# A two-layer streaming trunk on one core: output weight's sums tied to score steps one by one, and the final norm of a row block in two pieces

## The chip, the cores and the metric

The kernel runs on one core of a Trainium2 chip. The metric is the device time of one execution in microseconds, as a median over runs. Before the change it is 2714.26 us (three runs, 2712.99 to 2715.75). Matrix products run on TensorE (PE; its weight loads, PEld, are listed apart), elementwise work on VectorE (DVE), ScalarE (ACT) and GpSimd (POOL). Every DMA is issued by SyncE (SP), in the order of its queue.

## The reference

`x` has 2048 rows of 1024 numbers, all in float32. Layer A is a gated MLP with spatial mixing. Layer B, where the change lies, is attention of each 64-row chunk over its own and the eight chunks before it, with a bias by relative position, a SiLU gate and an output projection. A last RMS norm gives the result:

```
q, z = split(rms_norm(x, b_g) @ w_qz);   k, v = split(rms_norm(x, kv_g) @ w_kv)
p    = softmax(q k^T / 8 + bias[rel])    # per chunk of 64 rows, band of 576
o    = (p v) * silu(z)
x2   = x + o @ w_b_out
out  = x2 * rsqrt(mean(x2^2) + 1e-6) * final_norm_g
```

## The kernel before

**Tiling.** Layer B walks over four tiles t of 512 rows and, in each, over eight head pairs p (two heads of 64). One (t, p) has eight **steps** u = 0 to 7: two heads times four blocks of 128 query rows. Every product in float32 accuracy is made of three passes over a high and a low part (`mm3`, L112 to L116), so operands have to be split: ACT copies the high part, DVE subtracts it to get the low part.

**One step.** `score` (L1299) of a step two further on: PE multiplies queries with keys (L1314), DVE adds the bias and takes the row maximum (L1322), ACT takes the exponential (L1329), DVE the reciprocal of the sum (L1332), POOL scales the row (L1333). `flip` (L1338) of this step: PE transposes the five 128-column blocks of the row into the one PSUM buffer `tp` (L1349; its pool `ptr` has one buffer), ACT casts them into the high part of `pt` (L1352), DVE subtracts to the low part (L1353). Only then can PE transpose the next row. At two places of a pair `value` (L1358) multiplies the probabilities with the values. In tile 0 a row has 128 to 512 columns, from tile 1 on 640, so that the first 640-wide cast of L1352 is step 0 of tile 1, pair 0.

**What fills PE between the steps.** A generator (`ahead`, L1577) gives projections of the next pair and parts of the output projection of the tile before (`o_all`, L1552), in shares per pair (`SHARE`, L1558). The output projection is a Strassen-like product: seven phases, each with a weight matrix that is a sum or difference of quarters of the output weight.

**The sums of the output weight.** `o_sums` (L289) makes these seven matrices once, during tile 1, pairs 0 to 3 (a quarter of the columns in each pair). It loads four pieces `wo` (L296) and returns seven functions; the main loop calls one per step, at u = 0 to 6, just behind `flip` (L1637). Each calls `keep` (L299): ACT copies the high part (L303), DVE subtracts the low part (L304), SP stores both to DRAM (`ows`, L306; one phase also stores `owf`, L301). The first three also run sums on POOL: two (L310, L311), one (L315), one (L319). The high and low parts lie in a pool of four buffers (tag "S"), so two phases fit at once. The output projection of tile 0, from pair 4 on, reads `ows` (L231).

**The final norm.** When a 128-row block of x2 is complete, `done` (L1488) leaves a `finish` (L1504) in the list `finals`; the main loop calls the first one in each step with u > 0 (L1635), behind `flip`. `finish` adds two partial sums of squares (L1507), takes the inverse root (L126 to L128, on DVE and POOL), loads the block `y` from DRAM (L1513; the tag "bx" has one buffer), scales its two halves on DVE (L1516) and stores them (L1520). There are four such blocks for each of tiles 0, 1 and 2, finished in tiles 1, 2 and 3. For the last tile the rows stay on the chip and `finish` runs at once.

**What sets the order.** The lines above only say in which order instructions are written. When the program is built, the framework plans each engine's queue: with its own estimates of durations it puts an instruction into the queue as soon as its inputs and buffers are free by the plan, the earliest written one first. An instruction can so stand far ahead of where it was written. On the chip each queue runs strictly in the planned order and waits on semaphores for what it needs. A manual dependency without a semaphore (`NoSync`; `paced_by_pj`, L173, is one already) binds the plan alone: the instruction isn't placed before the named one is done by the plan.

Of the kernel before, what the change touches and what calls it, by code (L numbers as in the profile page):

```python
# [13 lines left out]
ALU = mybir.AluOpType  # L14
# [3 lines left out]
P = 128  # L18
# [3 lines left out]
T = 512  # L22
# [11 lines left out]
def trunk_kernel(  # L34
# [19 lines left out]
    nc = tc.nc  # L54
# [27 lines left out]
    ident = cst.tile([P, P], F32, name="ident")  # L82
# [27 lines left out]
    mm, tpose = nc.tensor.matmul, nc.tensor.transpose  # L110
# [12 lines left out]
    sub, add = ALU.subtract, ALU.add  # L123
    tv, tg = nc.vector.tensor_tensor, nc.gpsimd.tensor_tensor

    def root(r):  # L126
        nc.vector.tensor_scalar(r, r, EPS, None, op0=ALU.add)
        nc.gpsimd.tensor_tensor(r, r, mhalf[:], op=ALU.pow)  # L128
# [40 lines left out]
            tv(tl[:, :, b * P : (b + 1) * P], x3, oh.bitcast(F32), op=sub)  # L169

    pace = []

    def paced_by_pj(ins):  # L173
        if pace:
            tc.add_manual_dep(
                ins.ins, pace[-1],
                mybir.DependencyInfo(mybir.DependencyClass.NoSync, mybir.DependencyReason.DATA),
                reason="order",
            )
# [109 lines left out]
    def o_sums(u, place, s_place):  # L289

        q, i = divmod(u, 2)
        cs = slice(i * 512, i * 512 + 512)
        w = {}
        for rc in ((0, 0), (0, 1), (1, 1), (1, 0)):
            w[rc] = place(f"wo{u}_{rc[0]}{rc[1]}")
            paced_by_pj(nc.sync.dma_start(w[rc][:], wb_out[rc[0], rc[1], q][:, cs]))  # L296
        b11, b12, b21, b22 = (w[k][:] for k in ((0, 0), (0, 1), (1, 0), (1, 1)))

        def keep(ph, src):  # L299
            if ph == 5:  # L300
                nc.sync.dma_start(owf[q][:, cs], src)  # L301
            hi, lo = (s_place(f"so{u}_{ph}{x_}") for x_ in "hl")
            nc.scalar.copy(hi[:], src)  # L303
            tv(lo[:], src, hi[:].bitcast(F32), op=sub)  # L304
            for n, y_ in enumerate((hi, lo)):
                nc.sync.dma_start(ows[ph, q][:, n, cs], y_[:].bitcast(F32))  # L306

        def first():
            keep(1, b11)
            tg(b11, b12, b11, op=sub)  # L310
            tg(b12, b22, b12, op=sub)  # L311

        def second():
            keep(3, b22)
            tg(b22, b22, b11, op=sub)  # L315

        def third():
            keep(2, b21)
            tg(b21, b21, b22, op=sub)  # L319

        return [first, second, third] + [
            lambda ph=ph, o=o: keep(ph, o)
            for ph, o in ((5, b11), (7, b12), (6, b22), (4, b21))
        ]

    with ExitStack() as actx:
# [21 lines left out]
        sub, add, mul = ALU.subtract, ALU.add, ALU.mult  # L348
# [7 lines left out]
        last = {}  # L356
# [536 lines left out]
        for n in range(2, 6):  # L893
            b = start[n, 1]
# [46 lines left out]
        tv, tg = nc.vector.tensor_tensor, nc.gpsimd.tensor_tensor  # L941
# [259 lines left out]
    with ExitStack() as bctx:  # L1201
# [5 lines left out]
        gf = cb.tile([P, D], F32, name="gf")  # L1207
# [10 lines left out]
        def half_tile(tag, name, bufs, dtype=F32):  # L1218
            return sb.tile([P, 512], dtype, tag=tag, name=name, bufs=bufs)

        def c_tile(name):
            return half_tile("C", name, 4)
# [115 lines left out]
        def flip(t, p, u):  # L1338

            hd, qb = divmod(u, 4)  # L1340
            h = 2 * p + hd
            if qb == 0:
                pts[t, h] = sb.tile([P, 5376], F32R, tag="PT", name=f"pt{t}_{h}", bufs=1)
            pt = pts[t, h]
            pr = prs[t, h, qb]
            b0 = 0 if t > 0 else 4 - qb
            tp = ptr.tile([P, KD, P], F32, tag="tr", name=f"tp{t}_{h}_{qb}")
            for b in range(b0, 5):
                tpose(tp[:, b, :], pr[:, b * P : (b + 1) * P], ident[:])  # L1349
            o = qb * 640  # L1350
            oh = pt[:, o + b0 * P : o + 640]
            nc.scalar.copy(oh, tp[:, b0:5, :].rearrange("p a b -> p (a b)"))  # L1352
            nc.vector.tensor_tensor(  # L1353
                pt[:, 2560 + o + b0 * P : 2560 + o + 640],
                tp[:, b0:5, :].rearrange("p a b -> p (a b)"), oh.bitcast(F32), op=ALU.subtract,
            )
# [40 lines left out]
        finals = []  # L1397
# [74 lines left out]
        def o_evict(t):  # L1472
            xa, ya = {}, {}
            last = t + 1 == NT

            def resid(r, c, jp, x_):
                b = 2 * jp + r
                nc.sync.dma_start(x_, x1d[t][b * P : (b + 1) * P, c * 512 : c * 512 + 512])

            def place(r, c, jp):  # L1480
                if not last:
                    return c_tile(f"oc{t}_{r}{c}{jp}")[:]
                b = 2 * jp + r
                if b not in row:
                    row[b] = sb.tile([P, 2, 512], F32, tag="K", name=f"row{b}", bufs=4)
                return row[b][:, c, :]

            def done(r, c, jp, y):  # L1488
                b = 2 * jp + r
                if (t, b) not in ssq:  # L1490
                    ssq[t, b] = sm.tile([P, 2], F32, tag="ssq", name=f"ssq{t}_{b}", bufs=4)
                jk = c_tile(f"jk{t}_{r}{c}{jp}")
                nc.scalar.activation(
                    jk[:], y, AF.Square, scale=1.0 / 32, accum_out=ssq[t, b][:, c : c + 1]
                )
                if not last:
                    nc.sync.dma_start(x2d[t][b][:, c * 512 : c * 512 + 512], y)
                if (r, c) in ((1, 0), (0, 1)):
                    if last:
                        finish(b)  # L1500
                    else:
                        finals.append(lambda: finish(b))

            def finish(b):  # L1504
                r = sm.tile([P, 1], F32, tag="rr", name=f"rr_f{t}_{b}", bufs=4)
                s_ = ssq[t, b]
                tv(r[:], s_[:, 0:1], s_[:, 1:2], op=add)  # L1507
                root(r[:])
                if last:
                    y = row[b]  # L1510
                else:
                    y = sb.tile([P, 2, 512], F32, tag="bx", name=f"y{t}_{b}", bufs=1)
                    nc.sync.dma_start(y[:].rearrange("p a b -> p (a b)"), x2d[t][b][:])  # L1513
                for c in range(2):
                    cs = slice(c * 512, c * 512 + 512)
                    nc.vector.scalar_tensor_tensor(  # L1516
                        y[:, c, :], y[:, c, :], r[:], gf[:, cs], op0=ALU.mult, op1=ALU.mult
                    )
                    r0 = t * T + b * P
                    nc.sync.dma_start(out[r0 : r0 + P, cs], y[:, c, :])  # L1520

            def evict(ph, jp, ps):
                if ph in (1, 7):
                    d = xa if ph == 1 else ya
                    d[jp] = half_tile("U", f"ou{t}_{ph}_{jp}", 4)[:]
                    nc.scalar.copy(d[jp], ps)
                    return
                x_, y_ = xa[jp], ya[jp]
                if ph in (2, 5):
                    r = 0 if ph == 2 else 1  # L1530
                    c = place(r, r, jp)
                    resid(r, r, jp, c)
                    tv(c, ps, c, op=add)
                    tg(c, c, x_ if ph == 2 else y_, op=add)
                    done(r, r, jp, c)
                    if ph == 5:
                        tv(x_, ps, x_, op=add)
                        for r, c, y in ((1, 0, y_), (0, 1, x_)):
                            o = c_tile(f"or{t}_{r}{c}{jp}")[:]
                            resid(r, c, jp, o)  # L1540
                            tg(y, y, o, op=add)
                elif ph == 6:
                    tv(x_, ps, x_, op=add)
                    tg(y_, y_, x_, op=add)
                else:
                    r, c, y = (1, 0, y_) if ph == 4 else (0, 1, x_)
                    o = place(r, c, jp) if last else y
                    tv(o, ps, y, op=add)  # L1548
                    done(r, c, jp, o)
            return evict  # L1550
# [53 lines left out]
        first = ahead(0, 0)  # L1604
# [102 lines left out]
```

## Time and profile before

| | before |
|---|---|
| median of three runs | 2714.26 us |
| the profiled execution | 2716.97 us |
| its span, first to last instruction | 2715.2 us |
| mean granted TensorE clock | 0.988 |
| instructions | 38098 |

Times in the profile count from the start of the span. A row of the timeline gives the start, the duration, engine, line, operation, output and inputs, shapes, and in brackets the idle time of the engine just before, with what ended it. Attention takes the span from about 1540 us on; tile 1 begins near 1764 us, tile 2 near 2082 us, tile 3 near 2378 us.

### The profile page before, as it was taken

The page shows a single profiled execution, that of the slowest core. Times are in us where ns is not written, and L with a number is a line of the kernel's source. Part 1 is how long each engine was busy: PE and PEld are TensorE (multiplying, and loading weights), DVE is VectorE, ACT ScalarE, POOL GpSimd, SP SyncE. Part 2 cuts the span into 40 slices and gives each one's busy share as a digit, 9 for nine tenths or more (in the row PEclk, how much of TensorE's full clock was granted, in tenths as well). Part 3 has the DMA queues.
Part 4 walks back from the last instruction along what each step waited for, and adds up shares of the span by engine and source line. Part 5 has one row for each costly group of instructions (what it writes and reads, how often), then busy time and mean ns, then how long its engine had stood idle before and what let it go on. Part 6 is the DMA issues. An engine that isn't in the chain of part 4 may idle for free. (4 is left out here: it accounts for less than half of the span.)

```text
span 2715.2 us, 38098 instructions
## 1 busy us (share of the span) xinstructions
PE 2630.3 (97%) x12960; PEld 2195.9 (81%) x12960; DVE 1891.3 (70%) x2937; ACT 1296.8 (48%) x2296; POOL 892.1 (33%) x874
## 2 busy tenths in 40 slices
PE   9999999999999999999989999999999999999997
PEld 7788888888888888888878777787887888888875
DVE  6655676676677768667687666778667667766676
ACT  5422242433524435332365465666555565665553
POOL 3512235142351414114134243333332223223243
PEclk9999999999999999999999999999999999999999
DMA  8898999989988879768666677788778667766577
GB/s 302 309 334 333 349 354 328 328 308 352 325 308 299 294 263 344 252 222 298 241 215 226 210 255 222 233 287 272 260 261 286 213 211 239 243 205 198 182 228 244
DMA packets 274770, 735.53 MB, mean 271 GB/s; under 512 B 29584, under 2 KB 61328, under 8 KB 274576
## 3 DMA queue, kind: packets, MB, share of 16 engines
q1 hardware_dynamic: 274576, 733.09, 77.9%
q8 instruction: 104, 1.70, 0.3%
q14 instruction: 90, 0.74, 0.1%
HBM read 540.56 MB, written 181.93 MB: 266 GB/s over the span
## 5 line engine op out<-in xcount | busy, mean ns | idle before, releaser
L113 PE MATMUL P<-T,S 128*128 128x512 f32 x1248 | 495.2, 397 | 2.1 <-ACT S L376 2.1
L115 PE MATMUL P<-T,S 128*128 128x512 f32 x1248 | 489.3, 392 | 0.0
L114 PE MATMUL P<-T,S 128*128 128x512 f32 x1248 | 488.1, 391 | 0.6 <-DVE T L379 0.6
L1333 POOL TENSOR_SCALAR pr<-pr,sl 128x640 f32<-128x640 f32 (+4 forms) x256 | 198.2, 775 | 564.7 <-DVE sl L1332 494.5
L113 PE MATMUL pj<-hh_b,wh_b 128*128 128x512 f32 x768 | 322.2, 419 | 1.8 <-ACT hh_b L168 1.0
L115 PE MATMUL pj<-hh_b,wl_b 128*128 128x512 f32 x768 | 305.6, 398 | 0.3 <-DVE wl_b L200 0.2
L114 PE MATMUL pj<-hl_b,wh_b 128*128 128x512 f32 x768 | 305.6, 398 | 0.0
L1329 ACT ACTIVATE pr<-pr,nm 128x640 f32<-128x640 f32 (+4 forms) x256 | 195.4, 763 | 176.5 <-DVE nm L1322 170.8
L115 PEld LDWEIGHTS P<-T,S 128*128 128x128 f32 x1248 | 234.7, 188 | 50.2
L113 PEld LDWEIGHTS P<-T,S 128*128 128x128 f32 x1248 | 235.3, 189 | 46.8 <-ACT S L376 2.3
L114 PEld LDWEIGHTS P<-T,S 128*128 128x128 f32 x1248 | 235.2, 188 | 46.3 <-DVE T L379 1.0
L1353 DVE TENSOR_TENSOR pt<-tp,pt 128x640 fp32r<-128x640 f32 (+4 forms) x256 | 188.9, 738 | 60.1 <-ACT pt L1352 56.7
L1322 DVE CUSTOM_DVE_ANT_0 pr<-s,bias 128x640 f32<-128x640 f32 (+4 forms) x256 | 188.3, 735 | 38.5 <-PE s L1314 33.0
L1349 PE MATMUL tp<-ident,pr 128*128 128x128 f32 x1120 | 169.2, 277 | 26.9 <-DVE pt L1353 23.2
L1352 ACT CAST pt<-tp 128x640 fp32r<-128x640 f32 (+4 forms) x256 | 159.2, 622 | 64.5 <-PE tp L1349 60.4
L1349 PEld LDWEIGHTS tp<-ident,pr 128*128 128x128 f32 x1120 | 131.7, 142 | 62.6 <-issue 30.4
L115 PEld LDWEIGHTS pj<-hh_b,wl_b 128*128 128x128 f32 x768 | 146.1, 190 | 33.6 <-DVE wl_b L200 1.2
L1373 PEld LDWEIGHTS pv<-pt,V 128*128 128x128 f32 x896 | 144.9, 191 | 29.0 <-DVE pt L1353 7.9
L1373 PE MATMUL pv<-pt,V 128*128 128x256 f32 (+3 forms) x896 | 157.7, 323 | 7.3 <-DVE pt L1353 4.3
L113 PEld LDWEIGHTS pj<-hh_b,wh_b 128*128 128x128 f32 x768 | 147.1, 191 | 20.3 <-ACT wh_b L199 1.6
L114 PEld LDWEIGHTS pj<-hl_b,wh_b 128*128 128x128 f32 x768 | 147.1, 192 | 16.9
L200 DVE TENSOR_TENSOR wl_b<-raw_b,wh_b 128x1024 fp32r<-128x1024 f32 x96 | 122.8, 1280 | 33.2 <-ACT wh_b L199 32.0
(284 smaller groups left out, 5734.5 us busy)
## 6 DMA issues: line engine op xcount, KB each, us to landing
S<-hsd SPq DMA_DIRECT2D x288, 512.0 KB, 5.3
rw<-in_w_a SPq DMA_DIRECT2D x108, 512.0 KB, 6.2
A<-ytd SPq DMA_DIRECT2D x72, 512.0 KB, 5.8
raw_b<-wk SPq DMA_DIRECT2D x72, 512.0 KB, 4.3
hsd<-S SPq DMA_DIRECT2D x56, 512.0 KB, 4.4
V<-vhd SPq DMA_DIRECT2D x56, 512.0 KB, 5.2
wh_bo<-ows SPq DMA_DIRECT2D x50, 512.0 KB, 4.5
wl_bo<-ows SPq DMA_DIRECT2D x50, 512.0 KB, 5.6
```

Source lines behind the costliest of these rows:

```text
L113: first = mm(ps, lh, rh, start=first, stop=False)
L114: mm(ps, lh, rl, start=False, stop=False)
L115: mm(ps, ll, rh, start=False, stop=last)
L200: tv(wl[:], raw[:], wh[:].bitcast(F32), op=sub)
L1322: nc.vector.tensor_tensor_reduce(out=pr[:, c0:].rearrange("p (a b) -> p a b", a=nseg), in0=ps[:, :nseg, :w], in1=bias[:, c0:].rearrange("p ...
L1329: nc.scalar.activation(pr[:, c0:], pr[:, c0:], AF.Exp, scale=-1.0, bias=nm[:], accum_out=sl[:])
L1333: nc.gpsimd.tensor_scalar(pr[:, c0:], pr[:, c0:], sl[:], 1.0, op0=ALU.mult, op1=ALU.mult)
L1349: tpose(tp[:, b, :], pr[:, b * P : (b + 1) * P], ident[:])
L1352: nc.scalar.copy(oh, tp[:, b0:5, :].rearrange("p a b -> p (a b)"))
L1353: nc.vector.tensor_tensor(pt[:, 2560 + o + b0 * P : 2560 + o + 640], tp[:, b0:5, :].rearrange("p a b -> p (a b)"), oh.bitcast(F32), op=ALU ...
L1373: mm(po[:, q0 * P : q1 * P], vtl[t, p][:, i, hs], rhs, start=(i == blocks[0] and j == 0), stop=(i == 7 and j == 1),)
```

## The change

A list `beat` gets the name of the last transposition of each `flip`. `on_beat` gives an instruction a dependency without a semaphore on the newest entry: it isn't placed in its queue before that transposition is done by the plan. So tied are, in the sums, the ACT copy of each `keep` and the four POOL sums; the DVE subtraction and the stores follow from their data. In the final norm, for tiles 0 to 2, `finish` is cut in two: the addition (tied), the root and the load of `y` in one step, and the two scalings (tied) with their stores as a function `scale` that is put at the head of `finals`, and so called in the next step with u > 0. The load of `y` is not tied. For the last tile nothing changes. No instruction is added or taken away.

```
+    beat = []
+    def on_beat(ins):
+        if beat:
+            tc.add_manual_dep(
+                ins.ins, beat[-1],
+                mybir.DependencyInfo(mybir.DependencyClass.NoSync, mybir.DependencyReason.DATA),
+                reason="order",
+            )
+        return ins
...
-            nc.scalar.copy(hi[:], src)
+            on_beat(nc.scalar.copy(hi[:], src))
...
-            tg(b11, b12, b11, op=sub)
-            tg(b12, b22, b12, op=sub)
+            on_beat(tg(b11, b12, b11, op=sub))
+            on_beat(tg(b12, b22, b12, op=sub))
...
-                tpose(tp[:, b, :], pr[:, b * P : (b + 1) * P], ident[:])
+                ins = tpose(tp[:, b, :], pr[:, b * P : (b + 1) * P], ident[:])
+            beat.append(ins.ins.name)
...
-                tv(r[:], s_[:, 0:1], s_[:, 1:2], op=add)
+                first = tv(r[:], s_[:, 0:1], s_[:, 1:2], op=add)
                 root(r[:])
                 if last:
                     y = row[b]
                 else:
+                    on_beat(first)
                     y = sb.tile([P, 2, 512], F32, tag="bx", name=f"y{t}_{b}", bufs=1)
                     nc.sync.dma_start(y[:].rearrange("p a b -> p (a b)"), x2d[t][b][:])
-                for c in range(2):
...
+                def scale():
+                    for c in range(2):
+                        cs = slice(c * 512, c * 512 + 512)
+                        ins = nc.vector.scalar_tensor_tensor(
+                            y[:, c, :], y[:, c, :], r[:], gf[:, cs], op0=ALU.mult, op1=ALU.mult
+                        )
+                        if not last:
+                            on_beat(ins)
+                        r0 = t * T + b * P
+                        nc.sync.dma_start(out[r0 : r0 + P, cs], y[:, c, :])
+
+                if last:
+                    scale()
+                else:
+                    finals.insert(0, scale)
```

The two POOL sums of the second and third function (L315, L319) are tied in the same way.

More of the change, by code (lines that the diff above doesn't have):

```diff
@@ L309, in first @@
             keep(1, b11)
-            tg(b11, b12, b11, op=sub)
-            tg(b12, b22, b12, op=sub)
+            on_beat(tg(b11, b12, b11, op=sub))
+            on_beat(tg(b12, b22, b12, op=sub))
         def second():
             keep(3, b22)
-            tg(b22, b22, b11, op=sub)
+            on_beat(tg(b22, b22, b11, op=sub))
         def third():
             keep(2, b21)
-            tg(b21, b21, b22, op=sub)
+            on_beat(tg(b21, b21, b22, op=sub))
         return [first, second, third] + [
@@ L1511, in finish @@
                 else:
+                    on_beat(first)
                     y = sb.tile([P, 2, 512], F32, tag="bx", name=f"y{t}_{b}", bufs=1)
                     nc.sync.dma_start(y[:].rearrange("p a b -> p (a b)"), x2d[t][b][:])
-                for c in range(2):
[L1515 to L1520, printed above, removed]
+                def scale():
[12 more added lines that the diff above has]
+                    finals.insert(0, scale)
             def evict(ph, jp, ps):
```

## The prediction

> **What bounds the kernel now.** I read the page first, for the engine that is the bound, then the waits of that engine, then the timeline of the engines that it waits for.
>
> ```profile
> span 2715.2 us, 38098 instructions
> PE 2630.3 (97%) x12960; PEld 2195.9 (81%) x12960; DVE 1891.3 (70%) x2937; ACT 1296.8 (48%) x2296; POOL 892.1 (33%) x874
> L1349 PE MATMUL tp<-ident,pr 128*128 128x128 f32 x1120 | 169.2, 277 | 26.9 <-DVE pt L1353 23.2
> ```
>
> PE is the bound, busy for 97%. What can be won is its idle time, and in attention most of that stands before transpositions: there is one buffer `tp`, so a transposition waits until DVE has taken the row before out of it (L1353). Two stretches matter here, PE's waits while the sums are made (1735 to 1900 us) and while tile 1's final blocks are written (2290 to 2400):
>
> ```profile
> PE tp L1349 <- DVE pt L1353: 9.1, 4, 3.2
> ```
>
> ```profile
> PE tp L1349 <- DVE pt L1353: 6.0, 2, 3.1
> PE s L1314 <- DVE nm L1322: 0.6, 1, 0.6
> ```
>
> The sums cost 9.1 us in four gaps, the final blocks 6.0 in two and a remainder. The timeline has the larger five, and the windows of 6 us around each have the clock in the column behind the engines:
>
> ```profile
> 1805.55 0.52 PE L1349 MATMUL tp<-ident,pr 128*128 128x128 f32 x3 [2.11 <-DVE pt L1353]
> 1840.66 0.66 PE L1349 MATMUL tp<-ident,pr 128*128 128x128 f32 x2 [2.54 <-DVE pt L1353]
> 1877.23 0.41 PE L1349 MATMUL tp<-ident,pr 128*128 128x128 f32 x2 [3.18 <-DVE pt L1353]
> 2308.51 0.87 PE L1349 MATMUL tp<-ident,pr 128*128 128x128 f32 x3 [2.93 <-DVE pt L1353]
> 2345.06 0.41 PE L1349 MATMUL tp<-ident,pr 128*128 128x128 f32 x2 [3.11 <-DVE pt L1353]
> ```
>
> ```profile
> 1805.00:1811.00 6.00, 5.45 (x23) 4.71 (x24) 4.17 (x9) 2.30 (x5) 1.09 (x3) 0.72 0.96 311
> 1839.00:1845.00 6.00, 4.34 (x17) 3.87 (x18) 4.50 (x9) 2.63 (x5) 0.91 (x2) 0.72 0.76 221
> 1876.00:1882.00 6.00, 4.77 (x18) 4.13 (x19) 4.36 (x9) 1.87 (x4) 0.80 (x1) 0.72 0.67 210
> 2307.00:2313.00 6.00, 4.49 (x18) 3.96 (x19) 5.91 (x11) 2.21 (x4) 1.90 (x4) 0.72 0.70 192
> 2344.00:2350.00 6.00, 4.94 (x19) 4.32 (x20) 4.60 (x13) 2.12 (x5) 0.80 (x1) 0.72 0.68 205
> ```
>
> Each gap is followed by a low clock: 0.72 over 6 us is a loss of 6 x 0.28 = 1.7 us. So a gap costs its length and 1.7 us more. (The Trainium skill, "TensorE: Matmul & The Clock Gate", Part 1, halves the clock only after an idle window of about 3.4 us. These gaps are 2.1 to 3.2 us, and the clock fell at each: here the trace decides. By the page the five terms of 1.7 below would be nought and the forecast some 6 us smaller.)
>
> **Why the gaps at the sums.** They run far ahead of their steps and in bursts. ACT, from its timeline:
>
> ```profile
> 1746.68 0.61 ACT L303 CAST so_1h<-wo 128x512 fp32r<-128x512 f32 x1
> ...
> 1764.63 0.69 ACT L1352 CAST pt<-tp 128x640 fp32r<-128x640 f32 x1 [0.55 <-PE tp L1349]
> ...
> 1802.88 0.62 ACT L303 CAST so_6h<-wo 128x512 fp32r<-128x512 f32 x1 [1.68 <-DMA ows<-so_5h]
> ...
> 1839.63 0.62 ACT L303 CAST so_7h<-wo 128x512 fp32r<-128x512 f32 x1 [2.42 <-DMA ows<-so_2h]
> ```
>
> The first 640-wide cast, at 1764.63, is step 0 of tile 1, pair 0; the first sum was written behind it and stands 18 us ahead of it. The next rows show ACT held at a sum's copy (1.68, 2.42 us) until an earlier store frees a "S" buffer, with exponentials and casts behind it in the queue. On DVE, just before the gap at 1840.66:
>
> ```profile
> 1835.50 1.71 DVE L304 TENSOR_TENSOR so_2l<-wo,so_2h 128x512 fp32r<-128x512 f32 x1
> 1837.24 0.69 DVE L1383 TENSOR_TENSOR og<-pv,ot 64x512 f32<-64x512 f32 x1
> 1837.97 1.69 DVE L1390 SCALAR_TENSOR_TENSOR og<-og,Z 128x512 f32<-128x512 f32 x1
> 1839.69 0.82 DVE L1353 TENSOR_TENSOR pt<-tp,pt 128x640 fp32r<-128x640 f32 x1
> ```
>
> A subtraction of the sums (1.71) and the end of the pair before (0.69, 1.69) fill DVE until the subtraction that frees `tp` starts at 1839.69, and PE resumes a microsecond later.
>
> **Why the gaps at the final blocks.** DVE stands at the scaling until `y` has landed:
>
> ```profile
> 2306.16 1.41 DVE L1516 SCALAR_TENSOR_TENSOR y<-y,rr_f,gf 128x512 f32<-128x512 f32 x2 [4.44 <-DMA y<-x2d]
> ...
> 2340.89 2.44 DVE L1516 SCALAR_TENSOR_TENSOR y<-y,rr_f,gf 128x512 f32<-128x512 f32 x2 [1.73 <-DMA y<-x2d]
> ```
>
> Behind it in DVE's queue wait the subtractions that free `tp`: these are the gaps at 2308.51 and 2345.06.
>
> **The change, part by part.** Nothing is added or removed, so no engine's busy time changes but where instructions get in each other's way; all is order.
>
> *Sums, 28 functions.* Each copy now stands right behind the cast of its step's row in ACT's queue: it was tied to the transposition for which that cast waits too, so on ACT the tie costs nothing, even if it were a wait. The subtraction (0.69 us free) comes behind `pt` on DVE. Two stores of each, and one `owf` per pair, move with it on SP; they wait there for DVE, as now. The load of the next pair's `wo` comes later, since its buffers are held to steps 3 to 6; two steps are left until its use.
>
> What goes: all four gaps, 9.1 us, and three clock losses, 5.1: 14.2. What is late next: in pairs 1 to 3 DVE itself. In windows over these pairs (1803.41 to 1908.55), over stretches without a gap, and over one with many:
>
> ```profile
> 1803.41:1908.55 105.14, 96.77 (x521) 82.46 (x521) 83.30 (x147) 66.55 (x120) 34.76 (x45) 0.95 0.82 268
> ```
>
> ```profile
> 1908.00:1951.00 43.00, 43.00 (x233) 37.06 (x232) 27.45 (x48) 23.70 (x44) 10.75 (x15) 1.00 0.82 278
> 2041.00:2082.00 41.00, 37.15 (x196) 31.10 (x195) 33.94 (x64) 25.20 (x45) 11.49 (x15) 0.96 0.84 281
> 2225.00:2262.00 37.00, 37.00 (x205) 32.08 (x204) 27.60 (x50) 21.80 (x39) 12.63 (x16) 1.00 0.71 233
> ```
>
> DVE works 83.3 us there. Without the three gaps (7.8) and their clock (5.1) the stretch would be 105.1 - 12.9 = 92.2 us, DVE 90% busy. Where PE has no gap DVE is at 64% (27.45 of 43) or 75% (27.60 of 37); at 83% (33.94 of 41) PE already has gaps. ACT (66.55) and POOL (34.76 of 105.14) have room: that is what hides the copies (0.62 us) and POOL's sums; without it each copy would delay an exponential by its length. So I count half of these 12.9, 6.4 us (bounds 0 and 12.9, and below nothing in the rival C), and the whole first gap in pair 0, 9.1 - 7.8 = 1.3. Sum: 7.7.
>
> *Final blocks.* In tile 2 the first two scalings move behind the next step's transposition, about 4 us on, when `y` has landed (it landed at the end of each wait). What goes: 6.0 and two clocks, 3.4: 9.4. The scalings (1.41 us) then stand before another row's subtraction; I charge 0.5 us for each of the two, a third of it, since DVE has slack there: 8.4 (bounds 0 and 10.0 with the 0.6). In tile 1 the ties hardly bind: the first scaling there is tied to the last step of pair 6, and lies 8 us behind it already (cast and scaling, from two timelines):
>
> ```profile
> 2032.53 0.69 ACT L1352 CAST pt<-tp 128x640 fp32r<-128x640 f32 x1 [0.29 <-PE tp L1349]
> ```
>
> ```profile
> 2040.64 1.42 DVE L1516 SCALAR_TENSOR_TENSOR y<-y,rr_f,gf 128x512 f32<-128x512 f32 x2 [0.82 <-DMA y<-x2d]
> ```
>
> So nothing there, and nothing in tile 3, where the single buffer of `y` spaces the blocks in the same way (bounds for the two tiles: one gap with its clock, 3.6 us, either way). The load isn't tied and stays where it is; an SP queue that waits for a later scaling at its store (L1520) is the same wait moved by a step.
>
> Sum: 7.7 + 8.4 = 16.1 us, of 2716.97 us in the profiled execution (span 2715.2): 2700.9. The median before is 2.7 us lower, so a median of **2698 us** after.
>
> **The rivals.**
> A, the forecast: both halves work as above, 2698; with all of both (14.2 + 10.0) it is 2690, with two new gaps elsewhere (3.6 us each, below), since all queues are planned anew from 1746 us on, 2705.
>
> B, DVE becomes the bound in pairs 1 to 3. L304 there:
>
> ```profile
> 1803.41:1908.55 105.14, 13.84 (x16) 0.95 0.82 268
> ```
>
> If each of the 21 subtractions ran at 1.71 us, as so_2l does, DVE would need 83.3 - 13.8 + 35.9 = 105.4 us, the present length: the sums win only pair 0's 1.3, and with the final blocks' 8.4 the time is 2704.6. For it: one per step, they meet POOL's scaling of a row in every step. Against: sixteen took 13.84, 0.87 on average. (The Trainium skill, "SBUF — State Buffer", Who interferes with whom, says that a DVE instruction with two SBUF inputs is blocked by a GpSimd one that reads SBUF, and that the later one blocks fully: by that rule B.)
>
> C, slower: the wait for "S" buffers stays and is spread. A phase needs the buffers of two steps ago, whose stores must have landed. Two steps can be short, from 1764.63 above to 6.8 us on, and a store takes 4.6 us at the median and 10.1 at most, behind a subtraction and a place in SP's queue:
>
> ```profile
> 1771.39 0.69 ACT L1352 CAST pt<-tp 128x640 fp32r<-128x640 f32 x1
> ```
>
> ```profile
> DMA to landing us min/median/max: 2.3/4.6/10.1
> ```
>
> Each such wait stands before the next exponential. The present four gaps cost 14.2, 3.6 each; the saving at stake is 14.2 + 8.4 = 22.6, so from the seventh of 28 steps on (7 x 3.6 = 25) the kernel is slower. With 12 such steps it is 2714.3 + 43 - 22.6 = 2735. Against: most pairs of steps take 8 to 9 us (105.14 for 24 steps).
>
> D, the change does nothing that shows: new gaps in the replanned queues eat it, 2714.
>
> **How the numbers follow.** A 0.66, B 0.14, C 0.10, D 0.10. The likeliest is A: 2698 us. The range goes from a little below all of both, 2686, for a lucky replanning, to D's 2714; C and the rest below are left out. 0.2% (5.4 us) is about what a measurement of this kernel can tell from no change. Faster: A but 0.02, and 0.11 of B, 0.75. Slower: C and 0.03 of D, 0.13. Same: the rest, 0.12.
>
> **What would show it.** Right, if L303 rows stand one behind each 640-wide cast of L1352 in tile 1's first four pairs, without waits for `ows`; if PE's wait for `pt` in 1735 to 1900 falls from 9.1 to under 5; if DVE no longer waits for `y` in tile 2 and the gaps there are gone with their clock. Wrong, if L304 takes 1.7 us on most rows (B), if L303 waits for `ows` in seven steps or more (C), or if PE gaps of equal sum stand elsewhere (D).

## The result, and the profile after

The changed kernel takes 2704.94 us (median of 11 runs, 2699.51 to 2709.19), the kernel before 2714.26 (11 runs, 2708.07 to 2721.41): a ratio of 0.9964, with a 95% interval of 0.9952 to 0.9977. By the ratio that is a gain of 9.8 us (6.2 to 13.0 by the interval); the two medians are 9.3 us apart. Run again later (e10 below) it had a ratio of 0.9955 (0.9943 to 0.9967), 12.2 us. The forecast was 2698, a gain of 16.1; the time lies within the range and on the forecast side, and the gain is smaller than forecast.

The page after, with the same three rows as before. PE's idle time at the transpositions (the first figure behind the second bar) fell from 26.9 to 19.0 us. The program has 11 instructions more than before; none is among those counted for the five engines, whose counts are the same. In the new line numbering L303, L304 are L313, L314; L1349, L1352, L1353 are L1359, L1363, L1364; L1516 is L1530.

```profile
span 2703.8 us, 38109 instructions
PE 2625.2 (97%) x12960; PEld 2188.7 (81%) x12960; DVE 1887.0 (70%) x2937; ACT 1295.5 (48%) x2296; POOL 887.1 (33%) x874
L1359 PE MATMUL tp<-ident,pr 128*128 128x128 f32 x1120 | 168.4, 276 | 19.0 <-DVE pt L1364 13.1
```

Where the time went is read from windows. I cut both traces at the same casts, those of step 0: of tile 1 pair 0, of tile 1 pair 4 (the end of the sums), of tile 2, of tile 3. Each row has the stretch, its length, then busy time (and count) of PE, PEld, DVE, ACT and POOL, the granted clock, the DMA share and GB/s. First before, then after:

```profile
1764.63:1908.55 143.92, 133.98 (x720) 113.35 (x719) 114.47 (x203) 92.48 (x165) 51.35 (x62) 0.96 0.83 273
1908.55:2081.89 173.34, 167.52 (x877) 142.12 (x876) 123.63 (x221) 96.57 (x176) 57.32 (x69) 0.98 0.81 271
2081.89:2377.91 296.02, 288.17 (x1572) 248.57 (x1571) 211.90 (x391) 173.15 (x310) 92.73 (x121) 0.99 0.71 231
2377.91:2715.20 337.29, 313.32 (x1651) 263.96 (x1649) 233.41 (x415) 178.03 (x326) 106.94 (x133) 0.98 0.65 212
```

```profile
1764.34:1902.02 137.68, 130.33 (x713) 108.82 (x712) 112.59 (x203) 94.27 (x169) 52.97 (x65) 0.99 0.88 292
1902.02:2074.86 172.84, 165.20 (x875) 140.28 (x874) 126.06 (x223) 97.06 (x177) 55.17 (x68) 0.99 0.83 274
2074.86:2365.04 290.18, 285.93 (x1573) 245.90 (x1572) 213.02 (x390) 172.16 (x308) 92.69 (x120) 1.00 0.73 235
2365.04:2703.80 338.76, 314.67 (x1653) 264.46 (x1651) 233.24 (x417) 177.90 (x327) 108.14 (x135) 0.98 0.64 211
```

The sums' stretch is 6.2 us shorter, tile 2 is 5.8 shorter, the rest of tile 1 0.5 shorter, and tile 3 is 1.5 longer. The stretches end at the same casts, not at the same products: the sums' stretch has 713 matmuls in place of 720, and eight more stand ahead of it, where a gap of 1.24 us (at 1757.07 in the trace before, still in tile 0) is gone. DVE's busy time hardly moved; the clock rose in both stretches that the change touches. The second profile of the changed kernel gives 138.6, 169.0, 288.6 and 341.6 us: the two touched stretches come again, the other two don't (−4.3 and +4.3 against before), so single profiles say little about those.

PE's waits in the two stretches that the prediction quoted, of after (total, times, longest):

```profile
PE tp L1359 <- DVE pt L1364: 4.9, 6, 2.0
```

```profile
PE s L1324 <- DVE nm L1332: 2.1, 2, 1.6
PE tp L1359 <- POOL bias L1305: 0.9, 1, 0.9
PE tp L1359 <- DVE pt L1364: 0.6, 2, 0.4
```

The first row (1735 to 1900 us) stood at 9.1 us before; the last of the second view (2280 to 2390) at 6.0. In tile 2 other waits of 2.1 and 0.9 us came in, which were 0.6 and nothing. In the first window, too, PE's waits other than the row shown rose, from 3.0 to 5.0 us in all.

### The profile page after: what moved, and what is told of

Its sections match the earlier page's. It is cut to its first block, busy times and chain, and to the rows that moved or that the text cites. A ratio compares the mean times of both kernels' runs of the same rounds, so it can differ in the third digit from the quotient of the medians.

```text
span 2703.8 us, 38109 instructions
## 1 busy us (share of the span) xinstructions
PE 2625.2 (97%) x12960; PEld 2188.7 (81%) x12960; DVE 1887.0 (70%) x2937; ACT 1295.5 (48%) x2296; POOL 887.1 (33%) x874
## 4 chain that ended last, share of the span: by engine, by line
PE 77%; DVE 8%; DMA 7%; issue 3%; POOL 2%; ACT 2%; SPq 1%; DVEq 0%; POOLq 0%; ACTq 0%
PE P L115 11%; PE P L114 11%; PE P L113 11%; PE pj L113 5%; PE pj L115 5%; PE pj L114 5%; PE pv L1384 4%; PE s L1324 4%; PE tp L1359 3%; PE Po L115 2%; PE Po L113 2%; PE Po L114 2%; PE vp L115 2%; PE vp L114 2%; PE vp L113 2%
## 5 line engine op out<-in xcount | busy, mean ns | idle before, releaser
L1364 DVE TENSOR_TENSOR pt<-tp,pt 128x640 fp32r<-128x640 f32 (+4 forms) x256 | 188.8, 738 | 55.4 <-ACT pt L1363 52.1
L1363 ACT CAST pt<-tp 128x640 fp32r<-128x640 f32 (+4 forms) x256 | 159.1, 622 | 61.4 <-PE tp L1359 57.6
L1359 PE MATMUL tp<-ident,pr 128*128 128x128 f32 x1120 | 168.4, 276 | 19.0 <-DVE pt L1364 13.1
L1359 PEld LDWEIGHTS tp<-ident,pr 128*128 128x128 f32 x1120 | 130.8, 141 | 54.9 <-issue 22.3
L210 DVE TENSOR_TENSOR wl_b<-raw_b,wh_b 128x1024 fp32r<-128x1024 f32 x96 | 126.9, 1322 | 42.3 <-ACT wh_b L209 41.0
```

Of the source, the lines that this page charges most:

```text
L210: tv(wl[:], raw[:], wh[:].bitcast(F32), op=sub)
L1359: ins = tpose(tp[:, b, :], pr[:, b * P : (b + 1) * P], ident[:])
L1364: nc.vector.tensor_tensor(pt[:, 2560 + o + b0 * P : 2560 + o + 640], tp[:, b0:5, :].rearrange("p a b -> p (a b)"), oh.bitcast(F32), op=ALU ...
```

## The experiments

All eleven runs are compared by the same four stretches, in us. The last column is the time: for timed kernels the median and the ratio to the kernel before in the same set of runs, with its interval; for the others one execution. The lengths come from the same cuts as above, in each kernel's own trace. What stands ahead of tile 1 is not in the columns: it takes 1763.1 to 1766.7 us, but 1769.4 in e7.

| kernel | sums (tile 1, pairs 0-3) | rest of tile 1 | tile 2 | tile 3 to the end | time, ratio |
|---|---|---|---|---|---|
| before | 143.9 | 173.3 | 296.0 | 337.3 | 2714.26 |
| the changed kernel | 137.7 | 172.8 | 290.2 | 338.8 | 2704.94, 0.9964 [0.9952, 0.9977] |
| e10, the same again | 138.6 | 169.0 | 288.6 | 341.6 | 2706.22, 0.9955 [0.9943, 0.9967] |
| e1, sums alone | 138.4 | 171.6 | 296.6 | 337.9 | 2708.34, 0.9975 [0.9963, 0.9986] |
| e2, norm alone | 144.4 | 172.7 | 289.0 | 340.5 | 2713.8, 0.9992 [0.9982, 1.0003] |
| e3, three halves of y | 138.7 | 171.9 | 290.4 | 343.7 | 2710.38, 0.997 [0.9959, 0.9982] |
| e4, tie on the cast | 133.0 | 173.7 | 288.8 | 339.8 | 2701.46, 0.9946 [0.9934, 0.9959] |
| e11, the same again | 131.2 | 172.2 | 288.9 | 340.9 | 2704.63, 0.9947 [0.9934, 0.9961] |
| e9, cast, three steps | 135.6 | 172.8 | 287.6 | 338.1 | 2698.92, 0.9941 [0.9927, 0.9955] |
| e5, sums at step 0 | 141.7 | 172.9 | 290.6 | 340.4 | 2714.01, one execution |
| e6, norm split, untied | 138.8 | 169.0 | 291.6 | 337.7 | 2701.95, one execution |
| e7, norm tied, one piece | 139.9 | 174.3 | 295.2 | 338.4 | 2719.02, one execution |
| e8, no scaling | 138.3 | 166.9 | 288.5 | 338.9 | 2700.72, one execution |

The kernel before had medians of 2714.26 to 2718.9 us in these sets, so times of different sets are set side by side through their ratios only.

**e1: the sums alone.** The final norm as before, the rest as changed:

```
-                def scale():
...
-                    finals.insert(0, scale)
+                for c in range(2):
+                    ...
```

> The sums tied as in the change, the final norm in one piece and untied as before. Theory (two independent halves): tile 1, pairs 0 to 3, as in the changed kernel, 7.4 us shorter than before, and tile 2 with the two gaps of about 3 us at the scalings of the kernel before; in all 7 us under the kernel before, 2707. Rival (the gain is chance of the replanned queues): the stretch of the sums differs from the changed kernel's by 3 us or more, or the time is within 3 us of the kernel before.

Measured: 2708.34 us, a gain of 6.8 (3.8 to 10.0 by the interval). The sums' stretch is that of the changed kernel, tile 2 is as before. (The 7.4 us here and the 4.9 us in the next expectation are not differences of the table's columns, which give 6.2 and 5.8 for the changed kernel.) Its row for tile 2:

```profile
2075.03:2371.67 296.64, 288.67 (x1573) 248.67 (x1572) 213.00 (x391) 173.22 (x311) 92.96 (x121) 0.99 0.72 230
```

**e2: the norm alone.** The copies and POOL's sums without their ties:

```
-            on_beat(nc.scalar.copy(hi[:], src))
+            nc.scalar.copy(hi[:], src)
```

> The final norm in two tied pieces, the sums untied as before. Theory (two independent halves): the four gaps at the sums stay (9 us and three clock losses), tile 2 is 4.9 us shorter as in the changed kernel; in all 4 to 5 us under the kernel before, 2709.5. Rival (chance of the replanned queues): tile 2 differs from the changed kernel's by 2 us or more.

Measured: 2713.8 us, a gain of 2.2 (−0.8 to 4.9): not told from nothing. Its row for tile 2:

```profile
2082.43:2371.40 288.97, 285.76 (x1573) 245.79 (x1572) 213.41 (x390) 172.17 (x309) 91.45 (x120) 1.00 0.75 236
```

The sums' stretch is as before, tile 2 7.1 us shorter. The two halves act each on its own stretch, and the gains of e1 and e2 add up (9.0) to about that of the whole. But of the 7.1 us in tile 2 this profile lost 3.2 again in tile 3 (337.3 to 340.5).

**e3: three half buffers for y.** Two loads of half a block, each into one of three buffers, so that a load need not wait for the stores of the block before:

```
-                    y = sb.tile([P, 2, 512], F32, tag="bx", name=f"y{t}_{b}", bufs=1)
-                    nc.sync.dma_start(y[:].rearrange("p a b -> p (a b)"), x2d[t][b][:])
+                    y = [
+                        sb.tile([P, 512], F32, tag="bx", name=f"y{t}_{b}_{c}", bufs=3)
+                        for c in range(2)
+                    ]
+                    for c in range(2):
+                        nc.sync.dma_start(y[c][:], x2d[t][b][:, c * 512 : c * 512 + 512])
```

> The changed kernel with three buffers of half a row block for y in place of one of a whole, loaded in halves (a small pad tile is left out to make room). Theory Y (what tile 2, pair 7 didn't win is the single buffer: the load waits for the stores of the block before, so the last scaling still waits 1.7 us for y): the waits of DVE for y vanish, the PE gaps of 1.6 and 0.9 us in that pair too, 2 to 3 us less in tile 2 than the changed kernel, 2702. Rival D (DVE is the limit in that pair, with the reload of the next tile's rows): the waits for y vanish, but PE's gaps there stay at 3 us in sum and the time at 2705.

Measured: 2710.38 us. DVE still waits for a half in tile 2, 3.0 us once:

```profile
  DVE y L1534: 3.0, 1
```

Tile 2 is as in the changed kernel (290.4), tile 3 is 6.4 us longer than before. The edit didn't take away the wait that it was made for, so it settles nothing on that question.

**e4 and e11: the tie on the cast.** The beat is ACT's cast of the row in place of the last transposition:

```
-                ins = tpose(tp[:, b, :], pr[:, b * P : (b + 1) * P], ident[:])
-            beat.append(ins.ins.name)
+                tpose(tp[:, b, :], pr[:, b * P : (b + 1) * P], ident[:])
...
-            nc.scalar.copy(oh, tp[:, b0:5, :].rearrange("p a b -> p (a b)"))
+            ins = nc.scalar.copy(oh, tp[:, b0:5, :].rearrange("p a b -> p (a b)"))
+            beat.append(ins.ins.name)
```

> The changed kernel with every tie on ACT's cast of the step's row in place of the transposition, so that a copy of the sums can't be placed ahead of that cast. In the changed kernel several copies stand ahead of it, two at step 0 of pairs 1 and 3, where 1.4 and 2.0 us of PE gap are left. Theory E (the copies placed early bring DVE's subtractions early and cause these gaps): both gaps under 0.7 us, 4 to 5 us less than the changed kernel, 2700. Rival W (the gaps come from raw weights that land late, with DVE and ACT behind them): the gaps stay, 2704 to 2706.

> The changed kernel with its beat taken from ScalarE's cast in place of the last transposition (the same as e4_tie_cast), beside the changed kernel on one chip. Theory E, the place of the tie decides whether a sum's copy stands ahead of the cast or behind it and the lost gaps there cost some 3.5 us: 2 to 5 us under the changed kernel's time, and the stretch of the sums in the profile 2.5 to 4.5 us shorter than in the changed kernel. Rival, the first run of this edit was only a good placing of transfers: within 1.5 us of the changed kernel.

And the changed kernel beside e11, on one chip:

> The changed kernel as it is, once more, beside the kernel with its beat taken from the cast, on one chip. By both theories about 2705 if the kernel before is at 2714.3: a ratio to it of 0.9955 to 0.997.

Measured: the sums' stretch falls to 133.0 and 131.2 us, where seven profiles with the changed kernel's sums (its own two, e1, e3, e6, e7, e8) have 137.7 to 139.9; a third with this tie, e9 below, has 135.6. With the end one pair later the seven have 179.2 to 181.0 and the three 173.7 to 178.0 (before 186.4), so the order doesn't hang on where the stretch ends. The row of e11:

```profile
1763.53:1894.75 131.22, 127.09 (x712) 108.84 (x711) 111.35 (x205) 93.89 (x169) 52.24 (x65) 1.00 0.92 307
```

I had expected this because in the changed kernel copies stand ahead of the cast of their own step. ACT's timeline shows that they do: so_3h, of step 1, is at 1871.14, ahead of step 1's cast at 1873.28. But it also shows that the time was lost elsewhere. First ACT, then DVE, then PE of the changed kernel:

```profile
1868.35 1.05 ACT L209 CAST wh_b<-raw_b 128x1024 fp32r<-128x1024 f32 x1 [4.33 <-DMA raw_b<-wk]
...
1870.03 0.69 ACT L1363 CAST pt<-tp 128x640 fp32r<-128x640 f32 x1
1870.62 0.62 ACT L313 CAST so_1h<-wo 128x512 fp32r<-128x512 f32 x1
1871.14 0.62 ACT L313 CAST so_3h<-wo 128x512 fp32r<-128x512 f32 x1
1873.28 0.69 ACT L1363 CAST pt<-tp 128x640 fp32r<-128x640 f32 x1 [1.52 <-PE tp L1359]
```

```profile
1869.44 1.23 DVE L210 TENSOR_TENSOR wl_b<-raw_b,wh_b 128x1024 fp32r<-128x1024 f32 x1 [5.22 <-ACT wh_b L209]
1870.69 0.69 DVE L1394 TENSOR_TENSOR og<-pv,ot 64x512 f32<-64x512 f32 x1
1871.42 0.82 DVE L1364 TENSOR_TENSOR pt<-tp,pt 128x640 fp32r<-128x640 f32 x1
```

```profile
1872.39 0.85 PE L1359 MATMUL tp<-ident,pr 128*128 128x128 f32 x5 [2.02 <-DVE pt L1364]
```

Read backwards: PE stands 2.02 us until DVE has taken the row out of `tp` (1871.42); DVE came to it late. ACT's cast of that row (1870.03) stands behind the cast of a raw weight, which waited 4.33 us for the weight to land; on DVE the split of that weight (L210, after a wait of 5.22 us for ACT's cast) and an instruction of the pair before (L1394) stand ahead too. No sum is in this chain. The gap of 1.38 us at 1803.10 has the same chain, with a wait of 2.37 us for a weight. SP's queue says why the weight came late: its load stands behind the stores of a sum and the loads of the next quarter of `wo`.

```profile
1859.23 0.40 SPq L316 DMA_DIRECT2D ows<-so_4h  x1
1859.73 0.64 SPq L316 DMA_DIRECT2D ows<-so_4l  x1
1860.46 1.57 SPq L306 DMA_DIRECT2D wo<-in_wb_out  x2
1862.08 0.42 SPq L218 DMA_DIRECT2D raw_b<-wk  x1
...
1863.03 0.43 SPq L218 DMA_DIRECT2D raw_b<-wk  x1
```

It wasn't held by its two buffers: the last split before it (L210, at 1854.71, 1.22 us) had ended by 1856. In the kernel before, both loads for this place stand ahead of the loads of `wo`, and no cast waits for them:

```profile
1854.64 0.93 SPq L208 DMA_DIRECT2D raw_b<-wk  x2
...
1860.35 0.40 SPq L296 DMA_DIRECT2D wo<-in_wb_out  x1
```

At the same place in e11, ACT's and DVE's rows:

```profile
1858.86 0.69 ACT L1362 CAST pt<-tp 128x640 fp32r<-128x640 f32 x1
1859.45 0.62 ACT L313 CAST so_1h<-wo 128x512 fp32r<-128x512 f32 x1
1861.42 1.05 ACT L209 CAST wh_b<-raw_b 128x1024 fp32r<-128x1024 f32 x1 [1.35 <-DMA raw_b<-wk]
```

```profile
1859.58 0.82 DVE L1364 TENSOR_TENSOR pt<-tp,pt 128x640 fp32r<-128x640 f32 x1
```

Here the row's cast (1858.86) stands ahead of the weight's (1861.42), DVE takes the row out of `tp` at 1859.58, and PE has no gap. The weight's load is issued behind stores of a sum and four loads of `wo` in e11 too (at 1854.72): what the tie moved here is the order on ACT, not that on SP. ACT's waits for raw weights in the sums' stretch, of before, the changed kernel, e10 and e11:

```profile
ACT wh_b L199 <- DMA raw_b<-wk: 0.5, 1, 0.5
```

```profile
ACT wh_b L209 <- DMA raw_b<-wk: 7.3, 4, 4.3
```

```profile
ACT wh_b L209 <- DMA raw_b<-wk: 9.4, 5, 3.5
```

```profile
ACT wh_b L209 <- DMA raw_b<-wk: 3.0, 2, 1.7
```

It repeats: the seven profiles with the changed kernel's sums have 7.3 to 10.0 us of this wait, each with a gap of 1.2 to 2.8 us behind it at step 1 of pair 3; the three with the tie on the cast have 3.0 to 4.5, and the two with untied sums (before and e2) 0.5 and 0.3. So part of the gain became a new wait, for weights, and the tie on the cast makes it smaller and puts it where the row is already out. That the queues differ in this is shown; that this alone makes the 2 to 9 us between the two groups is not, since one tie moved replans every queue. Over the whole of tile 1 the groups touch: 303.4 to 308.4 us with this tie, 307.6 to 314.2 in six of the seven (e8 leaves out work there). In time the second pair of runs is 1.6 us apart on one chip (2704.63 and 2706.22), the first ratios 0.9946 and 0.9964, and all four intervals overlap: the shorter stretch is shown, a gain of the whole kernel by this edit is not.

**e5: the sums tied to step 0 of their pair.** All seven sums of a quarter may come as soon as step 0's transposition is done:

```
+    mark = []
...
-            on_beat(nc.scalar.copy(hi[:], src))
+            on_beat(nc.scalar.copy(hi[:], src), mark)
...
+            if u == 0:
+                mark.append(ins.ins.name)
```

> The changed kernel with all sums of a pair tied to the transposition of the pair's step 0, so that they can't run ahead of their pair but can come in a burst behind step 0. Theory S (the spreading, one per step, is what wins: ACT isn't held by stores and DVE isn't filled by a burst): the waits of ACT's copies for the stores come back (16.5 us in all before, 0.1 in the changed kernel; here over 8), and the stretch from tile 1, pair 0 to pair 4 is at least 4 us longer than in the changed kernel (137.7 us). Rival P (place: what wins is that the sums no longer meet the end of the pair before, og and its gate, on DVE): the stretch is within 2 us of the changed kernel's whatever the copies wait.

Measured: the sums' stretch is 141.7 us, 2.3 under before instead of 4.0 to 6.2. ACT stands at copies for stores again, 4.9 us in all, where it stood 12.6 before. One group of ACT's rows by form, of before, the changed kernel and e5 (the figure behind the second bar is the idle time in front):

```profile
L303 ACT CAST so_6h<-wo 128x512 fp32r<-128x512 f32 x4 | 2.5, 616 | 4.0 <-DMA ows<-so_5h 4.0
```

```profile
L313 ACT CAST so_6h<-wo 128x512 fp32r<-128x512 f32 x4 | 2.5, 616 | 0.0
```

```profile
L314 ACT CAST so_6h<-wo 128x512 fp32r<-128x512 f32 x4 | 2.5, 617 | 3.4 <-DMA ows<-so_5h 3.4
```

All seven such groups of the changed kernel show 0.0. Theory S had asked for more than 8 us of these waits and at least 4 us more than the changed kernel; it is 4.9, and 4.0 against one profile of the changed kernel and 3.1 against the other, so it came true by half; the rival's 2 us are exceeded. Holding the sums back to their pair takes most of the waits away (12.6 to 4.9), and spreading them over the steps takes the rest and wins the larger part of the stretch.

**e6 and e7: the split without ties, and the ties without the split.** In e6 the lines `on_beat(first)` and `on_beat(ins)` of the norm are left out; in e7 `scale()` is called at once:

```
-                if last:
-                    scale()
-                else:
-                    finals.insert(0, scale)
+                scale()
```

> The final norm's pieces as in the changed kernel (root and load in one step, scaling in the next), but without their ties to the transpositions; the sums as in the changed kernel. Theory S, the split alone takes the wait for y away and the ties of the norm add nothing: VectorE's waits for y in tile 2's pairs 6 and 7 come to less than 2.5 us in total (1.7 in the changed kernel, 6.8 before, 6.0 with the ties and one piece), tile 2 is 5 to 8 us shorter than before, the span 2701 to 2706. Rival T, the ties are needed too, since without them the scaling is put early in VectorE's queue and waits for its load: waits for y of 4 us or more, tile 2 at most 2.5 us shorter than before, the span 2707 to 2711.

> The changed kernel with the final norm tied but in one piece: addition, root, load, scaling and stores in one step. Theory L (the step between load and scaling is what wins, as y then has landed): DVE waits for y again 5 us or more in tile 2, with PE gaps of 2 to 3 us behind it, and tile 2 (pair 0 to tile 3, pair 1) is 4 to 5 us longer than in the changed kernel. Rival T (the tie alone puts the scaling late enough): tile 2 within 2 us of the changed kernel's.

Measured: tile 2 takes 291.6 us with the split alone, 295.2 with the ties alone (before 296.0, both together 288.6 to 290.2). DVE's waits for `y` there, of before, e6, e7 and the changed kernel:

```profile
DVE y L1516 <- DMA y<-x2d: 6.8, 3, 4.4
```

```profile
DVE y L1529 <- DMA y<-x2d: 3.8, 1, 3.8
```

```profile
DVE y L1530 <- DMA y<-x2d: 6.0, 3, 2.8
```

```profile
DVE y L1530 <- DMA y<-x2d: 1.7, 1, 1.7
```

In the changed kernel's second profile the wait is 0.2 us. The split does most of it, 4.5 us. Without the ties one scaling goes too early and waits 3.8 us for its load, which is the rival's mechanism in e6, at a price of 1 to 3 us; its numbers, 4 us of waits and at most 2.5 us won, did not come, nor did the theory's. The span of e6, 2700.2, was lower than either gave; the rest of tile 1 and tile 3 make that difference, on which one profile can't be relied. Theory L of e7 holds: the waits are back, and tile 2 is 5.1 and 6.7 us longer than in the changed kernel's two profiles.

**e8: no scaling.** In tiles 0 to 2 the multiplication of a row by its norm and gain (L1530) is left out; loads and stores stay:

```
-                        ins = nc.vector.scalar_tensor_tensor(
-                            y[:, c, :], y[:, c, :], r[:], gf[:, cs], op0=ALU.mult, op1=ALU.mult
-                        )
+                        if last:
+                            nc.vector.scalar_tensor_tensor(
+                                y[:, c, :], y[:, c, :], r[:], gf[:, cs], op0=ALU.mult, op1=ALU.mult
+                            )
```

> The changed kernel without the scaling in tiles 0 to 2: the blocks are loaded and stored as they are, the root is still taken (its output isn't the reference's in these rows). DVE is spared 24 scalings, 18 us, and no DVE instruction waits for y. Theory D (in the last pair of tile 2 the scalings and their wait on DVE are what still stands before PE): that pair's PE gaps (0.5, 0.9, 1.6 and 0.6 us) go to under 1 us in sum and tile 2 is 2 to 3 us shorter than in the changed kernel. Rival R (the reload of the next tile's rows, DVE and ACT work of its own, makes these gaps): 2 us of gaps stay.

Measured: tile 2 takes 288.5 us, 7.5 under before, and PE's gaps in its last pair come to 0.9 us. This is about what tile 2 has to give at the final blocks; the changed kernel has 5.8 of it in one profile and 7.4 in the other, so the scaling's own place in DVE's queue costs it 0 to 2 us. (The stretch of e8 holds 11 matmuls more. With the end one pair later the cost is 0.6 and 2.2 us.)

**e9: the cast, and an empty step between load and scaling.** e4 with

```
                     finals.insert(0, scale)
+                    if t + 2 < NT:
+                        finals.insert(0, lambda: None)
```

> The kernel with ties on the cast, and in tiles 1 and 2 a step left empty between a block's load and its scaling, so that a block takes three steps. Theory C (a block's load and store take some 11 us by the one buffer, two steps only 8 to 9, so the last block's load slips and DVE waits for it): no wait of DVE for y in tile 2, and 1 to 2 us less than the kernel with ties on the cast, 2700. Rival (the remaining gaps have other causes): time within 1 us of that kernel, or above it.

Measured: 2698.92 us, 0.9941 (0.9927 to 0.9955), the lowest median of all, 16 us under the kernel before. DVE has no wait for `y` in tile 2; but e4 and e11, without the empty step, have none either, so the wait that theory C was to take away was not there in this stretch. Tile 2 takes 287.6 us, 1.1 and 1.3 less than in those two. Against the changed kernel's first ratio the intervals overlap at the edge only; against its second, and against e4 and e11, they overlap more. It beats the kernel before clearly; that it beats e4 and e11 is not shown.

## Why the prediction was right, and where it was not

*What bounds the kernel, and where it can be won.* Right. Both gains are in the stretches that were named, and e1 and e2 move one each.

*The sums, 7.7 us: the total nearly right, the parts and the reason wrong.* Alone they bring 6.8 us (3.8 to 10.0), and 4.0 to 6.2 in the stretch over seven profiles. The store waits went as said. But the half that was deducted in pairs 1 to 3, 6.4 of 12.9 us, was deducted for DVE, which "90% busy" was to be late next. It wasn't. In e11 PE runs through pair 1 without a gap and at the full clock while DVE is busy for 27.47 of 30.91 us, 89%:

```profile
1797.25:1828.16 30.91, 30.91 (x178) 26.81 (x177) 27.47 (x51) 22.86 (x41) 12.55 (x17) 1.00 0.94 307
```

What was late in the changed kernel is the raw weights: ACT waits 7.3 and 9.4 us for them against 0.5 before. Pairs 1 to 3 take 101.3 us there, 9 more than the 92.2 without the old gaps; the two gaps behind weights (1.38 and 2.02 us) and the clock after the second (1.7) are 5.1 of these 9, and the rest was not taken apart (PE's smaller waits, and 526 matmuls in place of 521). The step that failed is "what is late next: in pairs 1 to 3 DVE itself"; it looked at busy time, and the next wait was a transfer behind the moved stores and loads in SP's queue, of which the prediction said only that they "wait there for DVE, as now". That the total came near is partly luck: in the seven profiles pairs 1 to 3 win 2.0 to 3.9 us, not 6.4, and pair 0 wins 2.0 to 3.2. The 1.3 us that the prediction counted for pair 0 are the gap at 1757.07, which lies ahead of that pair.

*"Each copy now stands right behind the cast of its step's row."* Wrong: the tie names the transposition, and the plan may put a copy ahead of the cast that waits for that transposition too. The row at 1871.14 shows it.

*The final blocks, 8.4 us.* The mechanism is right: the wait for `y` fell from 6.8 to 1.7 us (0.2 in the second profile), the two gaps before transpositions, 6.0 us, have shrunk to 0.6, and the clock is at 1.00. The size is off: 5.8 and 7.4 us in tile 2, 7.1 in e2 (with the end one pair later 5.0, 6.6 and 6.2). The charge of 0.5 us for each scaling that comes behind another row was too small in the profiled execution: the last block's load still landed late, DVE waited for it, and PE for DVE behind it (first DVE, then PE, of after):

```profile
2354.87 1.41 DVE L1530 SCALAR_TENSOR_TENSOR y<-y,rr_f,gf 128x512 f32<-128x512 f32 x2 [1.71 <-DMA y<-x2d]
...
2357.03 0.82 DVE L1332 CUSTOM_DVE_ANT_0 pr<-s,bias 128x640 f32<-128x640 f32 x1
```

```profile
2357.92 0.57 PE L1324 MATMUL s<-K,Qh 128*128 128x320 f32 x2 [1.56 <-DVE nm L1332]
```

*"Nothing in tile 3", bounds 3.6 us either way.* As a gain of the whole kernel the norm timed alone is worth 2.2 us (−0.8 to 4.9), which leaves out 8.4 and even the 7.1 of its own tile 2. In e2's profile 3.2 us are lost in tile 3. Of ten profiles with the norm's split tile 3 is longer than before in every one, by 0.4 to 6.4 us; without it (e1, e7) by 0.6 and 1.1, so the groups overlap. One place repeats in most of them, a wait of a transposition for POOL near the end, of before and of after:

```profile
2638.62 0.76 PE L1349 MATMUL tp<-ident,pr 128*128 128x128 f32 x4 [2.61 <-POOL pr L1333]
```

```profile
2627.51 0.90 PE L1359 MATMUL tp<-ident,pr 128*128 128x128 f32 x3 [3.85 <-POOL pr L1343]
```

In both, POOL is at sums for the last tile's output projection (`A_hl`, until 2637.78 before and 2626.16 after) just ahead of the row's scaling. The scalings of the norm don't cause this wait: e8, without them, has 3.90 us of it. Why tile 3 is longer stays open: before was profiled once, and no kernel was made for this stretch.

*The rivals.* B (DVE is the bound) fell: L314 takes 22.02 us for 28 in the sums' stretch, 0.79 each, less than the 0.87 before, though single ones still take 1.6. The window of L314 alone, of after:

```profile
1764.34:1902.02 137.68, 22.02 (x28) 0.99 0.88 292
```

C (the copies' waits stay and are spread) fell: they are at 0.0, though the steps are less even than C's counter-argument had it (from a cast to the next but one it took 5.7 to 13.8 us before; 8 to 9 is only the mean). The nearest to C is e5, with 4.9 us. D (new gaps eat it) is true in part: the wait for weights and the new gaps in tile 2 are such gaps, and they took about half of what the sums could give, not all.

*The signs.* The waits for `ows` are gone, and PE's wait is 4.9 us, just under its five. But DVE still waits for `y` in tile 2, and not every copy stands behind its cast.

## What to carry to other kernels

When work is spread out, look not only at how busy its engine becomes but at what its DMAs now stand ahead of in the queue that issues them: here the next wait was for a weight whose load had come behind moved transfers and whose cast stood ahead of a row's, and no busy time showed it. A tie binds only against the instruction that it names: what must stand behind a row's cast has to be tied to the cast, not to what the cast waits for. And a gain in one stretch of one profile is not yet a gain of the kernel: a part that gave 7.1 us in its stretch was worth 2.2 when timed, with an interval that includes zero.

## What the runs showed of the hardware

A gap of PE does not always cost the clock behind it. The prediction charged 1.7 us for each. After the gap of 2.02 us at 1872.39 in the changed kernel the clock was 0.72 over 6 us, as in the five gaps before. In e1 the same gap comes again, at 1872.29 and behind the same wait for a weight, and the clock after it was full; so it was after gaps of 2.30 us, in e8 at 1873.92 and in e6 at 2296.64. First the 6 us at the changed kernel's gap, then at e1's, with the gap itself:

```profile
1872.00:1878.00 6.00, 5.61 (x25) 4.84 (x26) 4.87 (x11) 3.55 (x6) 4.31 (x3) 0.72 0.75 248
```

```profile
1872.00:1878.00 6.00, 5.71 (x33) 4.86 (x33) 6.00 (x14) 4.94 (x9) 4.42 (x4) 1.00 0.78 264
```

```profile
1872.29 0.74 PE L1359 MATMUL tp<-ident,pr 128*128 128x128 f32 x5 [2.02 <-DVE pt L1364]
```

Over all thirteen profiles, from tile 1 on, the clock in the 6 us from 0.5 us ahead of PE's return was either 1.00 or 0.50 to 0.73. It was low after 21 of 53 gaps of 1.5 to 2.0 us, after 24 of 36 of 2.0 to 2.85, and after all 15 longer ones (a few of these windows hold a second gap). So below 2.85 us length alone doesn't decide, and the charge is a chance for gaps of this size. The Trainium skill, "TensorE: Matmul & The Clock Gate", Part 1, calls the window of about 3.4 us free-running; by that, where a gap falls in the window would matter, which fits these rows, while gaps as short as 2.02 us costing the clock does not fit its one idle window. No run here was made to tell more.
